# A two-layer hybrid mixer on one core: the first layer's U projection unsplit, norm sums ahead, and a new order of its parts

## The chip, the core and the metric

The kernel runs on one core of a Trainium2 chip. The metric is the device time of one execution in microseconds. Before the change it is 915.59 us, the median of three runs (913.13 to 916.24).

## What is computed

Two layers act on x (256 positions, 1024 channels). Each layer is a hybrid mixer and a gated convolutional feed-forward block, each behind an RMS norm and added to x. Cut to what matters here:

```
h = rmsnorm(x, norm_mix)
u, q, k_cmp, v_cmp, k_sel, v_sel, k_win, v_win, nsa_gate, g_ssm, g_nsa = split(h @ w_in)
y_ssm = s5_mixer(u) @ w_branch_ssm
y_nsa = nsa_mixer(rope(q), ...) @ w_branch_nsa
x = x + (sigmoid(g_ssm) * y_ssm + sigmoid(g_nsa) * y_nsa) @ w_out
x = x + conv_ffn(rmsnorm(x, norm_ffn))
```

The state-space mixer `s5_mixer` runs a linear complex recurrence over 256 steps for 32 groups of 64 states, with a GLU behind it. The attention `nsa_mixer` has 8 query heads on 2 key heads, and adds three softmax branches with gates: over 15 compressed blocks, over selected blocks (all four are selected at this length) and over a window longer than the sequence.

## The kernel before, in words

All activations lie transposed: channels on partitions, 256 positions along the free axis. Weights stream from one packed array `wst` in chunks of 128 x 1024 f32 (512 KB) through a ring of five `raw` buffers (L137, NRAW). Precision is kept in two ways. `split` (L144) turns a chunk into a high part `wh` (ScalarE, L148) and a rest `wl` (VectorE, L150), both fp32r, and `mm3` (L157) adds three fp32r matmuls. In the first layer's mixer most projections instead use the raw chunk in plain f32 matmuls against `xg`, the norm's input times its gain (`proj`, L407); there only U, the state-space input, is split. `split` needs a split input too, `ah` and `al`, made by `Norm.part` (L365, L368).

A norm works as follows: ScalarE squares the eight row blocks of x through one buffer `sq`, VectorE adds them into `nacc`; `finish` (L373) sums over partitions by small matmuls into `ps_n`, does a reciprocal square root in some fifteen tiny VectorE steps (`nt`), spreads it with another matmul, and ScalarE copies it to `rb` (L398). Projections are scaled by `rb` (or by rope tables `rc` that contain it) after the matmul, so matmuls need not wait for the norm.

The first layer's mixer then runs parts that a hand-written list, ORDER[0] (L54), puts in order: `par`, `pf`, `tb` (VectorE: parameters and rotation tables `E` of the recurrence), `q`, `kc`, `ks`, `v` (projections, the first three with rope, whose swapped halves go by DMAs `sw`), `mb` and `mc` (the recurrence's B and C), `cin`, `cw`, `ck`, `cv` (compressed blocks), `ac` and `at` (compressed softmax `sc` and its transpose `ps_ct`), `as` (scores, exponentials), `av` (transposes, values, output `oo`), and `g` (two gate projections and a tanh, eight pairs). A bare number in the list runs that many of sixteen recurrence steps, held in the sequence "A0 B0 A1 C0 B1 D0 A2 C1 B2 D1 A3 C2 B3 D2 C3 D3" (L608): A is the input matmuls `psb` and the products `bc`, `bs`, `z`; B and C are scans of the two halves of time; D the products `pr`, the output matmuls `psy` and the gelu. `gh` is a gate pair that may be issued on TensorE only behind the last attention score traced before it (`gates_held`).

The kernel is written with a tile library. At build time its planner goes through a timeline of its own and gives each engine the ready instruction with the highest priority; priority is the order of the program text. So ORDER sets priorities, and each engine then executes a fixed sequence in order. PSUM has two "mm" banks (projections, gates) and six "aux" banks (the rest). U's first two sums take both "mm" banks, the other two "aux" banks. Later in the mixer x is loaded again into the buffer that q used (L848), on the same SP queue as the weights.

Of the kernel before, what the change touches and what calls it, by code (L numbers as in the profile page):

```python
# [14 lines left out]
T = 256  # L15
# [24 lines left out]
for _name, _w in [("ropec", 256), ("ropes", 256), ("ident", 128), ("causal", 128),  # L40
# [10 lines left out]
NRAW, NWH, NWL, NSS, NSW, NRT, NPT, NZ, NTH = 5, 3, 3, 4, 1, 2, 2, 2, 8  # L51
AHEAD = (3, 4, 5, 6)

ORDER = [[int(x) if x.isdigit() else x for x in o.split()] for o in (  # L54
    ('par tb:0 pf q:1 q:0 mb kc cin tb:1 ks v g:0 1 g:1 cw:0:0 cw:0:1 1 cw:0:2 cw:0:3 1 ck mc 1 g:2 cw:1:0 cw:1:1 1 1 '
     'cw:1:2 cw:1:3 cv g:3 as:0:0 1 ac:0 at:0 1 av:0:0 g:4 as:0:1 1 1 ac:1 at:1 av:0:1 1 as:1:0 1 as:1:1:1 1 gh:5 1 '
     'av:1:0 1 gh:6 av:1:1 1 gh:7 '),
    ('kc mb q:1 1 1 cin 1 cw:0:0 cw:0:1 q:0 ks v 1 cw:0:2 cw:0:3 1 ck cw:1:0 1 ac:0 as:0:0 1 1 cw:1:1 cw:1:2 '
     'cw:1:3 cv g:1 g:2 1 at:0 av:0:0 as:0:1 1 av:0:1 ac:1 as:1:0 1 g:4 1 at:1 as:1:1:1 1 av:1:0 1 g:5 g:7 g:0 1 '
     'g:3 g:6 av:1:1 '))]  # L60
# [22 lines left out]
def body(tc, ctx, d, out):  # L83
# [260 lines left out]
    class Norm:  # L344
        def __init__(self, l, gname, x):
            self.x = x
            self.g = sp(l, gname)
            self.ah = pp.tile([128, KD, T], F32R, name="ah", tag="ah")
            self.al = pp.tile([128, KD, T], F32R, name="al", tag="al")
            self.acc = wk.tile([128, T], F32, name="nacc", bufs=1)  # L350
# [14 lines left out]
        def part(self, k, square=True):  # L365

            gk = self.g[:, k:k + 1]
            S.activation(self.ah[:, k, :], self.x[:, k, :], AF.Copy, scale=gk)  # L368
            stt(self.al[:, k, :], self.x[:, k, :], gk, self.ah[:, k, :].bitcast(F32), OP.mult, OP.subtract)
            if square:  # L370
                self.square(k)
# [29 lines left out]
    def mixer(l, nm, sc, first, mp, sm_):  # L401
        ah, al = nm.ah, nm.al
# [12 lines left out]
        if l == 0:  # L415
            xg = mp.tile([128, KD, T], F32, name="xg", bufs=1)
            for k in range(KD):
                S.activation(xg[:, k, :], nm.x[:, k, :], AF.Copy, scale=nm.g[:, k:k + 1])


        uy = []
        for h in range(2):
            cu = [c or split(l, f"u{2 * h + i}") for i, c in enumerate(first[2 * h:2 * h + 2])]
            psu = [bank("psu", ("mm", "aux")[h]) for _ in range(2)]
            for k in range(KD):
                for i in range(2):
# [99 lines left out]
        def ssm_a(q):  # L526

            Bh, Bl = sv["B"]
            Ec, Es = sv["sc"][:, 0], sv["sc"][:, 1]
            rt = mp.tile([128, 4, TC], F32, name="rm", tag="rm", bufs=1)  # L530
            G.tensor_copy(rt, par[:, R, sl0 + 4 * q:sl0 + 4 * q + 4, None].to_broadcast([128, 4, TC]))
            G.memset(rt[:, :, 0:1], 0.0)
            z = mp.tile([128, 2, 2, 4, TC], F32, name="z", tag="z", bufs=NZ)
            for h in range(2):
                psb = [bank("psb", "aux") for _ in range(2)]
                with row():
                    for c in range(2):
                        for w, y in ((Bh, 0), (Bh, 1), (Bl, 0)):
                            for a in range(2):
                                r = slice(64 * h + 32 * a, 64 * h + 32 * a + 32)  # L540
                                PE.matmul(psb[a][:, c * T:(c + 1) * T], w[r, q, c, :], uy[q][r, y, :],
                                          start=(w is Bh and y == 0), stop=(w is Bl), skip_group_check=True)
                bc = mp.tile([128, 2, 2, 2, TC], F32, name="bc", tag="sb", bufs=2)
                bs = mp.tile([128, 2, 2, 2, TC], F32, name="bs", tag="sb", bufs=2)
                for a in range(2):
                    j = 4 * q + 2 * h + a
                    src = psb[a].rearrange("p (r t) -> p r t", t=TC)
                    for o, e in ((bc, Ec), (bs, Es)):
                        tt(o[:, a].rearrange("p r c t -> p (r c) t"), src,
                           e[:, j, None, :].to_broadcast([128, 4, TC]), OP.mult)  # L550
                for c, op in ((0, OP.add), (1, OP.subtract)):
                    tt(z[:, :, c, 2 * h:2 * h + 2, :].rearrange("p k a t -> p a k t"), bc[:, :, c], bs[:, :, 1 - c], op,
                       eng("z", h))
            st[q] = z, rt
# [23 lines left out]
        def ssm_d(q):  # L578

            z, rt = st.pop(q)  # L580
            Ec, Es = sv["sc"][:, 0], sv["sc"][:, 1]
            Cm = sv["C"]
            psy = bank("psy", "aux")
            for i, (c, e, ci) in enumerate(((0, Ec, 0), (1, Es, 1), (0, Es, 2), (1, Ec, 2))):
                prs = []
                for h in range(2):
                    pr = lt.tile([128, 2, 2, TC], F32, name="pr", tag="ss", bufs=NSS)
                    j = 4 * q + 2 * h
                    tt(pr, z[:, :, c, 2 * h:2 * h + 2, :].rearrange("p k a t -> p a k t"),
                       e[:, j:j + 2, None, :].to_broadcast([128, 2, 2, TC]), OP.mult, eng("pr", 2 * i + h))  # L590
# [17 lines left out]
        ssm = [lambda f=dict(A=ssm_a, B=ssm_b2, C=ssm_c2, D=ssm_d)[o[0]], q=int(o[1]): f(q)  # L608
               for o in "A0 B0 A1 C0 B1 D0 A2 C1 B2 D1 A3 C2 B3 D2 C3 D3".split()]

# [104 lines left out]
        def a_s(qt, ih, alt=0):  # L715
# [4 lines left out]
            Ps = {}  # L720
            if alt:
                pb = [pp.tile([128, 2, 2, T], F32, name="pb", tag=t) for t in ("Bh", "Bl")]
            su = sm_.tile([128, 2, 2, 2], F32, name="su")
            for i2 in range(2):
                i = 2 * ih + i2
                svs = [bank("ps_s", "aux")[:, :2 * nk].rearrange("p (b k) -> p b k", b=2) for _ in range(2)]
                with row():
                    for w, y in ((0, 0), (0, 1), (1, 0)):
                        for kv in range(2):
                            r = slice(64 * kv, 64 * kv + 64)  # L730
                            PE.matmul(svs[kv], q[r, w, i, qs], ksw[r, y, :, :nk], start=(w + y == 0), stop=False,
                                      skip_group_check=True)
                    for kv in range(2):
                        at["hold"] = PE.matmul(svs[kv][:, :, nk - 128:], identb, causb, start=False, stop=True,
                                               skip_group_check=True)
                for kv in range(2):
                    sv = svs[kv]
                    mx = sm_.tile([128, 2], F32, name="mx2", bufs=3)
                    V.tensor_reduce(mx, sv, axis=AX.X, op=OP.max)
                    ts(mx, mx, -SCALE, OP.mult)  # L740
                    pt = pb[kv][:, i2] if alt else lt.tile([128, 2, nk], F32, name="pt", tag="pt", bufs=4)
                    for b in range(2):
                        S.activation(pt[:, b, :], sv[:, b, :], AF.Exp, bias=mx[:, b:b + 1], scale=SCALE,
                                     accum_out=su[:, kv, i2, b:b + 1])
                    Ps[kv, i2] = pt
            V.reciprocal(su, su)
            tt(su, su, gv[:, :, 2 * ih:2 * ih + 2, 1:3], OP.mult)
            for i2 in range(2):
                for kv in range(2):
                    for b in range(2):  # L750
                        S.activation(Ps[kv, i2][:, b, :], Ps[kv, i2][:, b, :], AF.Copy, scale=su[:, kv, i2, b:b + 1])
            at["P", qt, ih] = Ps

        def a_v(qt, ih):
            Ps = at.pop(("P", qt, ih))
# [29 lines left out]
        def gates(m):  # L785
            ps = proj2((f"g{m}", f"g{8 + m}"))
# [5 lines left out]
        def gates_held(m):  # L792

            with tc.issue_after(at["hold"].ins):
                gates(m)

        ssm.reverse()
        run = lambda n: [ssm.pop()() for _ in range(n) if ssm]
        for item in ORDER[l]:
            if isinstance(item, int):  # L800
                run(item)
            else:
                f, *a = item.split(":")
                {"kc": p_kc, "ks": p_ks, "q": p_q, "v": p_v, "cin": c_in, "cw": c_w1, "ck": c_k, "cv": c_v,
                 "par": p_par, "pf": p_pf, "tb": p_tb, "mb": p_mb, "mc": p_mc, "ac": a_cmp, "at": a_cmpt, "as": a_s, "av": a_v, "g": gates, "gh": gates_held}[f](*map(int, a))
        run(99)
# [315 lines left out]
```

## Time and profile before

| what | value |
|---|---|
| median of 3 runs | 915.59 us |
| profiled execution | 911.35 us |
| its span, first to last instruction | 909.6 us |
| TensorE matmul busy | 819.8 us, 90% |
| VectorE busy | 696.8 us, 77% |
| ScalarE busy | 429.4 us, 47% |
| mean granted TensorE clock | 0.94 |

The profile is of one execution. PE is TensorE's matmuls, PEld its weight loads, DVE VectorE, ACT ScalarE, POOL GpSimd, SP the queue that issues most DMAs. "PEclk" or the granted clock is the share of the full TensorE clock that was granted. Shares of the whole span hide that the stages differ; the rows further down are cut by stage. Matmul ends are modelled and overlap, so the price of one in a dense stretch is read from the distance of starts, or from a merged piece divided by its count.

### The profile page before, as it was taken

The page shows a single profiled execution, that of the slowest core. Times are in us where ns is not written, and L with a number is a line of the kernel's source. Part 1 is how long each engine was busy: PE and PEld are TensorE (multiplying, and loading weights), DVE is VectorE, ACT ScalarE, POOL GpSimd, SP SyncE. Part 2 cuts the span into 40 slices and gives each one's busy share as a digit, 9 for nine tenths or more (in the row PEclk, how much of TensorE's full clock was granted, in tenths as well). Part 3 has the DMA queues.
Part 4 walks back from the last instruction along what each step waited for, and adds up shares of the span by engine and source line. Part 5 has one row for each costly group of instructions (what it writes and reads, how often), then busy time and mean ns, then how long its engine had stood idle before and what let it go on. Part 6 is the DMA issues. An engine that isn't in the chain of part 4 may idle for free.

```text
span 909.6 us, 16504 instructions
## 1 busy us (share of the span) xinstructions
PE 819.8 (90%) x6488; PEld 741.9 (82%) x6488; DVE 696.8 (77%) x1337; ACT 429.4 (47%) x795; POOL 29.6 (3%) x58
## 2 busy tenths in 40 slices
PE   4799795789898999999999879997689999999994
PEld 4688574457798999999999748974389999999994
DVE  7975957575499999887784999978468788888553
ACT  6110122455346376565652224776445565655440
POOL 0000100000000000000000122100000000000000
PEclk9899785579999999999999999997899999999997
DMA  7155640024365566665874475332045565555641
GB/s 276 66 168 170 233 147 0 1 76 157 116 177 163 167 194 202 189 193 180 274 245 137 128 270 175 108 125 70 1 139 185 184 201 197 188 197 195 189 136 47
DMA packets 41774, 142.44 MB, mean 157 GB/s; under 512 B 5216, under 2 KB 6752, under 8 KB 41696
## 3 DMA queue, kind: packets, MB, share of 16 engines
q1 hardware_dynamic: 39712, 139.15, 47.7%
q10 hardware_dynamic: 1984, 2.23, 0.9%
q8 instruction: 51, 0.84, 0.4%
q14 instruction: 27, 0.22, 0.1%
HBM read 136.38 MB, written 2.10 MB: 152 GB/s over the span
## 4 chain that ended last, share of the span: by engine, by line
PE 75%; DVE 14%; ACT 4%; DMA 3%; issue 3%; POOL 0%; DVEq 0%; SPq 0%; ACTq 0%
PE ps_f L161 9%; PE ps_f L159 9%; PE ps_f L160 9%; PE ps_g L407 6%; PE ps_fo L160 4%; PE ps_fo L159 4%; PE ps_fo L161 4%; DVE z L561 2%; PE ps_q L407 2%; DMA raw<-wst 2%; PE psy L594 2%; PE ps_g L161 2%; PE ps_br L159 2%; PE ps_br L160 2%; PE ps_br L161 2%
## 5 line engine op out<-in xcount | busy, mean ns | idle before, releaser
L148 ACT CAST wh<-raw 128x1024 fp32r<-128x1024 f32 (+1 forms) x203 | 211.5, 1046 | 215.2 <-PE ps_f L160 96.4
L150 DVE TENSOR_TENSOR wl<-raw,wh 128x1024 fp32r<-128x1024 f32 (+1 forms) x203 | 247.5, 1222 | 64.2 <-ACT wh L148 63.4
L160 PE MATMUL ps_f<-al,wh 128*128 128x256 f32 x704 | 194.5, 276 | 2.3 <-DVE al L203 2.3
L159 PE MATMUL ps_f<-ah,wh 128*128 128x256 f32 x704 | 194.6, 277 | 1.2 <-DVE x L203 1.2
L161 PE MATMUL ps_f<-ah,wl 128*128 128x256 f32 x704 | 194.3, 276 | 0.0
L160 PEld LDWEIGHTS ps_f<-al,wh 128*128 128x128 f32 x704 | 132.2, 188 | 2.5 <-DVE al L203 2.5
L159 PEld LDWEIGHTS ps_f<-ah,wh 128*128 128x128 f32 x704 | 132.2, 188 | 1.3 <-ACT wh L148 1.3
L161 PEld LDWEIGHTS ps_f<-ah,wl 128*128 128x128 f32 x704 | 132.1, 188 | 0.0
L160 PE MATMUL ps_fo<-fl,wh 128*128 128x256 f32 x352 | 97.0, 276 | 0.0
L159 PE MATMUL ps_fo<-fh,wh 128*128 128x256 f32 x352 | 96.9, 276 | 0.0
L161 PE MATMUL ps_fo<-fh,wl 128*128 128x256 f32 x352 | 96.7, 276 | 0.0
L159 PEld LDWEIGHTS ps_fo<-fh,wh 128*128 128x128 f32 x352 | 66.1, 188 | 0.0
L160 PEld LDWEIGHTS ps_fo<-fl,wh 128*128 128x128 f32 x352 | 66.1, 188 | 0.0
L161 PEld LDWEIGHTS ps_fo<-fh,wl 128*128 128x128 f32 x352 | 65.9, 188 | 0.0
L407 PE MATMUL ps_g<-xg,raw 128*128 128x256 f32 x256 | 63.9, 409 | 1.0 <-DMA raw<-wst 1.0
L407 PEld LDWEIGHTS ps_g<-xg,raw 128*128 128x128 f32 x256 | 51.6, 206 | 11.1 <-issue 1.6
L194 DVE TENSOR_TENSOR pr<-z,E 128x512 f32<-128x512 f32 x64 | 41.9, 701 | 15.0 <-PE psy L594 14.9
L203 DVE SCALAR_TENSOR_TENSOR cv<-ab,sp,cv 128x255 f32<-128x255 f32 (+1 forms) x88 | 42.0, 480 | 1.4
L161 PE MATMUL ps_g<-ah,wl 128*128 128x256 f32 x128 | 38.0, 297 | 2.7 <-DVE wl L150 2.7
L561 DVE TENSOR_TENSOR_SCAN z<-rm,z 128x512 f32<-128x512 f32 x32 | 37.9, 1213 | 3.2 <-POOL z L194 3.1
L159 PE MATMUL ps_g<-ah,wh 128*128 128x256 f32 x128 | 37.2, 291 | 0.0
L160 PE MATMUL ps_g<-al,wh 128*128 128x256 f32 x128 | 36.6, 286 | 0.0
(264 smaller groups left out, 1754.5 us busy)
## 6 DMA issues: line engine op xcount, KB each, us to landing
raw<-wst SPq DMA_DIRECT2D x248, 512.0 KB, 4.2
x<-xT SPq DMA_DIRECT2D x4, 512.0 KB, 5.1
raw<-wst SPq DMA_DIRECT2D x4, 420.0 KB, 3.7
xd<-x SPq DMA_DIRECT2D x2, 512.0 KB, 6.9
x<-xd SPq DMA_DIRECT2D x2, 512.0 KB, 7.2
sw<-rt SPq DMA_DIRECT2D x12, 64.0 KB, 3.3
sw<-rt ACTq DMA_DIRECT2D x12, 64.0 KB, 3.4
raw<-wst SPq DMA_DIRECT2D x2, 280.0 KB, 2.7
```

Of the source, the lines that this page charges most:

```text
L148: S.copy(h[:, :n], t[:, :n])
L150: V.tensor_tensor(lo[:, :n], t[:, :n], h.bitcast(F32)[:, :n], op=OP.subtract)
L159: PE.matmul(ps, wh, ah, start=start, stop=False, **k)
L160: PE.matmul(ps, wh, al, start=False, stop=False, **k)
L161: PE.matmul(ps, wl, ah, start=False, stop=stop, **k)
L194: return e.tensor_tensor(o, a, b, op=op)
L203: e.scalar_tensor_tensor(o, a, s, b, op0=op0, op1=op1)
L407: PE.matmul(ps, w[:, k * 128:(k + 1) * 128], xg[:, k, :], start=k == 0, stop=k == KD - 1, skip_group_check=True)
L561: V.tensor_tensor_scan(f, rt.rearrange("p a t -> p (a t)"), f, 0.0, op0=OP.mult, op1=OP.add)
L594: PE.matmul(psy[32 * a:32 * a + 32, :T], Cm[:, ci, 4 * q + a, :], prs[a // 2][:, a % 2].rearrange("p c t -> p (c t)"), start=(i == 0), sto ...
```

## The change

The first layer's U projection uses raw chunks and `xg` in plain f32 like the others, all four sums in "aux" banks; `ah` and `al` are not made for that norm. Its squares come behind the `xg` copies, and its `finish` gets a priority 400 instructions earlier (0 in the second layer). The recurrence steps become named parts in ORDER, and A, D, the scores and the gates are cut in halves that can be placed by themselves. The first layer's order is new; the diff's core:

```diff
+HP = (400, 0)
-ORDER = [[int(x) if x.isdigit() else x for x in o.split()] for o in (
-    ('par tb:0 pf q:1 q:0 mb kc cin tb:1 ks v g:0 1 g:1 cw:0:0 cw:0:1 1 cw:0:2 cw:0:3 1 ck mc 1 g:2 cw:1:0 cw:1:1 1 1 '
-     'cw:1:2 cw:1:3 cv g:3 as:0:0 1 ac:0 at:0 1 av:0:0 g:4 as:0:1 1 1 ac:1 at:1 av:0:1 1 as:1:0 1 as:1:1:1 1 gh:5 1 '
-     'av:1:0 1 gh:6 av:1:1 1 gh:7 '),
-    ('kc mb q:1 1 1 cin 1 cw:0:0 cw:0:1 q:0 ks v 1 cw:0:2 cw:0:3 1 ck cw:1:0 1 ac:0 as:0:0 1 1 cw:1:1 cw:1:2 '
-     'cw:1:3 cv g:1 g:2 1 at:0 av:0:0 as:0:1 1 av:0:1 ac:1 as:1:0 1 g:4 1 at:1 as:1:1:1 1 av:1:0 1 g:5 g:7 g:0 1 '
-     'g:3 g:6 av:1:1 '))]
+ORDER = [o.split() for o in (
+    ('par tb:0 pf q:1 q:0 mb kc cin tb:1 A:0:0 A:0:1 ks B:0 v A:1:0 A:1:1 g:0:0 g:0:1 g:1:0 g:1:1 cw:0:0 cw:0:1 '
+     'C:0 cw:0:2 cw:0:3 ck mc B:1 D:0:0 D:0:1 g:2:0 g:2:1 cw:1:0 cw:1:1 A:2:0 A:2:1 cw:1:2 cw:1:3 cv ac:0 at:0 '
+     'ac:1 as:0:0:0 as:0:0:1 at:1 C:1 g:3:0 g:3:1 B:2 D:1:0 D:1:1 av:0:0 as:0:1:0 as:0:1:1 A:3:0 A:3:1 g:4:0 g:4:1 '
+     'av:0:1 as:1:0:0 as:1:0:1 C:2 g:5:0 g:5:1 B:3 as:1:1:0:1 as:1:1:1:1 D:2:0 D:2:1 av:1:0 g:6:0 g:6:1 C:3 g:7:0 '
+     'g:7:1 D:3:0 D:3:1 av:1:1 '),
+    ('kc mb q:1 A:0:0 A:0:1 B:0 cin A:1:0 A:1:1 cw:0:0 cw:0:1 q:0 ks v C:0 cw:0:2 cw:0:3 B:1 ck cw:1:0 D:0:0 D:0:1 '
+     'ac:0 as:0:0:0 as:0:0:1 A:2:0 A:2:1 C:1 cw:1:1 cw:1:2 cw:1:3 cv g:1:0 g:1:1 g:2:0 g:2:1 B:2 at:0 av:0:0 '
+     'as:0:1:0 as:0:1:1 D:1:0 D:1:1 av:0:1 ac:1 as:1:0:0 as:1:0:1 A:3:0 A:3:1 g:4:0 g:4:1 C:2 at:1 as:1:1:0:1 '
+     'as:1:1:1:1 B:3 av:1:0 D:2:0 D:2:1 g:5:0 g:5:1 g:7:0 g:7:1 g:0:0 g:0:1 C:3 g:3:0 g:3:1 g:6:0 g:6:1 av:1:1 '
+     'D:3:0 D:3:1 '))]
...
+            for k in range(KD):
+                nm.square(k)
...
-            cu = [c or split(l, f"u{2 * h + i}") for i, c in enumerate(first[2 * h:2 * h + 2])]
-            psu = [bank("psu", ("mm", "aux")[h]) for _ in range(2)]
+            cu = [c or (split(l, f"u{2 * h + i}") if l else raw(l, f"u{2 * h + i}"))
+                  for i, c in enumerate(first[2 * h:2 * h + 2])]
+            psu = [bank("psu", "aux" if l == 0 else ("mm", "aux")[h]) for _ in range(2)]
             for k in range(KD):
                 for i in range(2):
+                    if l == 0:
+                        PE.matmul(psu[i][:, :T], cu[i][0][:, k * 128:(k + 1) * 128], xg[:, k, :], start=k == 0,
+                                  stop=k == KD - 1, skip_group_check=True)
+                        continue
                     wh, wl = wt(cu[i], k)
                     mm3(psu[i][:, :T], wh, wl, ah[:, k, :], al[:, k, :], k == 0, k == KD - 1)
             if h == 0:
-                nm.finish()
+                with tc.high_priority(offset=HP[l]):
+                    nm.finish()
...
-        def gates(m):
-            ps = proj2((f"g{m}", f"g{8 + m}"))
+        def gates(m, h=None):
+            if h != 1:
+                th[m] = bank("ps_g")
+            ps = th[m]
+            for i in (0, 1) if h is None else (h,):
+                n = f"g{8 * i + m}"
+                proj(ps[:, i * T:(i + 1) * T], raw(l, n)[0] if l == 0 else split(l, n))
+            if h == 0:
+                return
...
-    nm = Norm(0, "g_mix", x)
-    first = [split(0, "u0")]
+    nm = Norm(0, "g_mix", x, False)
+    first = [raw(0, "u0")]
     nc.sync.dma_start(x[:, 4:8, :], d["xT"][:, 4:8, :])
-    first += [split(0, "u1"), None, None]
+    first += [raw(0, "u1"), None, None]
...
-    for k in range(KD):
-        nm.part(k, False)
-    for k in range(KD):
-        nm.square(k)
```

`ssm_a(q, h)`, `ssm_d(q, h)` and `a_s(qt, ih, i2)` get an argument for the half in the same way; their instructions stay as they are.

## Rows read from the trace of the kernel before

**Rows 1.** Stretches, in us from the start: length, busy time (instructions) per engine, PEclk, DMA.
```profile
0.00:21.00 21.00, 9.19 (x48) 8.19 (x48) 14.91 (x61) 14.17 (x29) 0.20 (x4) 1.00 0.76 271
21.00:35.57 14.57, 7.67 (x61) 7.18 (x61) 12.80 (x96) 1.94 (x5) 0.80 (x2) 0.91 0.29 107
35.57:70.20 34.63, 34.63 (x158) 29.60 (x158) 26.92 (x75) 4.79 (x10) 0.00 (x0) 0.94 0.46 137
70.20:135.00 64.80, 58.52 (x342) 45.32 (x342) 44.77 (x74) 10.36 (x22) 5.14 (x12) 0.89 0.57 187
135.00:195.00 60.00, 39.01 (x221) 24.93 (x222) 41.54 (x91) 21.35 (x76) 2.26 (x10) 0.56 0.00 0
195.00:227.00 32.00, 32.00 (x200) 24.41 (x200) 16.16 (x33) 21.45 (x53) 0.00 (x0) 0.97 0.50 165
227.00:235.00 8.00, 7.93 (x62) 5.25 (x61) 3.92 (x12) 2.37 (x6) 0.00 (x0) 1.00 0.19 66
...
490.00:660.00 170.00, 148.10 (x1191) 117.20 (x1192) 138.16 (x240) 87.25 (x193) 18.24 (x26) 0.93 0.38 121
...
70.20:235.00 164.80, 137.45 (x820) 99.91 (x821) 106.40 (x207) 55.52 (x156) 7.41 (x22) 0.79 0.33 109
```

**Rows 2.** Timeline, 25 to 52 us: start, length, engine, line, operation, idle before and releaser.
```profile
25.78 1.22 DVE L155 TENSOR_TENSOR Bl<-raw,Bh 128x1024 fp32r<-128x1024 f32 x1 [1.77 <-ACT Bh L154]
...
27.16 0.15 DVE L200 TENSOR_SCALAR nt<-ps_n 128x2 f32<-128x2 f32 x1
...
33.58 0.37 ACT L398 COPY rb<-ps_n 128x256 f32<-128x256 f32 x1 [7.84 <-PE ps_n L395]
...
35.57 16.11 PE L407 MATMUL ps_q<-xg,raw 128*128 128x256 f32 x64 [2.02 <-DVE uf L194]
```

**Rows 3.** Groups by line, 0 to 35.57 us: operation, count, busy and mean ns, idle before.
```profile
L150 DVE TENSOR_TENSOR wl<-raw,wh 128x1024 fp32r<-128x1024 f32 x4 | 4.9, 1222 | 0.1
L148 ACT CAST wh<-raw 128x1024 fp32r<-128x1024 f32 x4 | 4.0, 1038 | 0.2 <-DMA raw<-wst 0.2
...
L203 DVE SCALAR_TENSOR_TENSOR al<-x,sp,ah 128x256 fp32r<-128x256 f32 x8 | 3.5, 482 | 0.0
L368 ACT ACTIVATE ah<-x,sp 128x256 fp32r<-128x256 f32 x8 | 3.4, 493 | 0.0
```

**Rows 4.** Timeline of TensorE: split U at two times, one gate pair in plain f32.
```profile
13.31 0.41 PE L160 MATMUL psu<-al,wh 128*128 128x256 f32 x1
...
13.95 0.41 PE L160 MATMUL psu<-al,wh 128*128 128x256 f32 x1
...
19.11 0.28 PE L160 MATMUL psu<-al,wh 128*128 128x256 f32 x1
...
19.45 0.28 PE L160 MATMUL psu<-al,wh 128*128 128x256 f32 x1
...
74.86 7.17 PE L407 MATMUL ps_g<-xg,raw 128*128 128x256 f32 x32
```

**Rows 5.** Chain (first chunk), stretch 5 to 10 us, DMA issues with us to landing.
```profile
1.18 6.19 DMA raw<-wst
...
5.00:10.00 5.00, 0.58 (x1) 0.29 (x1) 3.89 (x16) 3.75 (x9) 0.00 (x0) 1.00 1.02 408
...
raw<-wst SPq DMA_DIRECT2D x248, 512.0 KB, 4.2
```

**Rows 6.** Timeline of ScalarE: two squares in a row.
```profile
5.84 0.40 ACT L357 ACTIVATE sq<-x 128x256 f32<-128x256 f32 x1
...
6.73 0.42 ACT L357 ACTIVATE sq<-x 128x256 f32<-128x256 f32 x1 [0.49 <-DVE nacc L194]
```

**Rows 7.** Waits of TensorE, 60 to 236 us: total, times, longest.
```profile
PE ps_ct L710 <- DVE sc L194: 15.4, 2, 9.5
```

**Rows 8.** Groups by line of TensorE, 195 to 235 us: the gate matmuls.
```profile
L407 PE MATMUL ps_g<-xg,raw 128*128 128x256 f32 x96 | 22.8, 392 | 0.0
```

**Rows 9.** Waits of the SP queue, 0 to 236 us: total, times, longest.
```profile
SPq L848 <- PE ps_s L734: 62.8, 1, 62.8
```

More of the change, by code (lines that the diff above doesn't have):

```diff
@@ L344, in body, with __init__ @@
     class Norm:
-        def __init__(self, l, gname, x):
+        def __init__(self, l, gname, x, split=True):
             self.x = x
             self.g = sp(l, gname)
-            self.ah = pp.tile([128, KD, T], F32R, name="ah", tag="ah")
-            self.al = pp.tile([128, KD, T], F32R, name="al", tag="al")
+            if split:
+                self.ah = pp.tile([128, KD, T], F32R, name="ah", tag="ah")
+                self.al = pp.tile([128, KD, T], F32R, name="al", tag="al")
             self.acc = wk.tile([128, T], F32, name="nacc", bufs=1)
@@ L363, in square, with part @@
                     self.rest = sq
-        def part(self, k, square=True):
+        def part(self, k):
             gk = self.g[:, k:k + 1]
@@ L369, in part @@
             stt(self.al[:, k, :], self.x[:, k, :], gk, self.ah[:, k, :].bitcast(F32), OP.mult, OP.subtract)
-            if square:
-                self.square(k)
+            self.square(k)
         def finish(self):
@@ L401, in mixer @@
     def mixer(l, nm, sc, first, mp, sm_):
-        ah, al = nm.ah, nm.al
+        if l:
+            ah, al = nm.ah, nm.al
         def proj(ps, w):
@@ L524, in mixer, with ssm_a @@
         ys = []
-        def ssm_a(q):
+        def ssm_a(q, h):
             Bh, Bl = sv["B"]
             Ec, Es = sv["sc"][:, 0], sv["sc"][:, 1]
[L530 to L554, printed above, removed]
@@ new lines, in ssm_a @@
+            if h == 0:
+                rt = mp.tile([128, 4, TC], F32, name="rm", tag="rm", bufs=1)
+                G.tensor_copy(rt, par[:, R, sl0 + 4 * q:sl0 + 4 * q + 4, None].to_broadcast([128, 4, TC]))
+                G.memset(rt[:, :, 0:1], 0.0)
+                st[q] = mp.tile([128, 2, 2, 4, TC], F32, name="z", tag="z", bufs=NZ), rt
+            z = st[q][0]
+            psb = [bank("psb", "aux") for _ in range(2)]
+            with row():
+                for c in range(2):
+                    for w, y in ((Bh, 0), (Bh, 1), (Bl, 0)):
+                        for a in range(2):
+                            r = slice(64 * h + 32 * a, 64 * h + 32 * a + 32)
+                            PE.matmul(psb[a][:, c * T:(c + 1) * T], w[r, q, c, :], uy[q][r, y, :],
+                                      start=(w is Bh and y == 0), stop=(w is Bl), skip_group_check=True)
@@ new lines, in ssm_a @@
+            bc = mp.tile([128, 2, 2, 2, TC], F32, name="bc", tag="sb", bufs=2)
+            bs = mp.tile([128, 2, 2, 2, TC], F32, name="bs", tag="sb", bufs=2)
+            for a in range(2):
+                j = 4 * q + 2 * h + a
+                src = psb[a].rearrange("p (r t) -> p r t", t=TC)
+                for o, e in ((bc, Ec), (bs, Es)):
+                    tt(o[:, a].rearrange("p r c t -> p (r c) t"), src,
+                       e[:, j, None, :].to_broadcast([128, 4, TC]), OP.mult)
+            for c, op in ((0, OP.add), (1, OP.subtract)):
+                tt(z[:, :, c, 2 * h:2 * h + 2, :].rearrange("p k a t -> p a k t"), bc[:, :, c], bs[:, :, 1 - c], op,
+                   eng("z", h))
@@ L576, in ssm_c2, with ssm_d @@
             scan(q, 1)
-        def ssm_d(q):
-            z, rt = st.pop(q)
+        def ssm_d(q, h):
+            z, rt = st[q]
             Ec, Es = sv["sc"][:, 0], sv["sc"][:, 1]
             Cm = sv["C"]
-            psy = bank("psy", "aux")
-            for i, (c, e, ci) in enumerate(((0, Ec, 0), (1, Es, 1), (0, Es, 2), (1, Ec, 2))):
+            if h == 0:
+                sv["psy"] = bank("psy", "aux")
+            psy = sv["psy"]
+            for i, (c, e, ci) in list(enumerate(((0, Ec, 0), (1, Es, 1), (0, Es, 2), (1, Ec, 2))))[2 * h:2 * h + 2]:
                 prs = []
-                for h in range(2):
+                for b in range(2):
                     pr = lt.tile([128, 2, 2, TC], F32, name="pr", tag="ss", bufs=NSS)
-                    j = 4 * q + 2 * h
-                    tt(pr, z[:, :, c, 2 * h:2 * h + 2, :].rearrange("p k a t -> p a k t"),
-                       e[:, j:j + 2, None, :].to_broadcast([128, 2, 2, TC]), OP.mult, eng("pr", 2 * i + h))
+                    j = 4 * q + 2 * b
+                    tt(pr, z[:, :, c, 2 * b:2 * b + 2, :].rearrange("p k a t -> p a k t"),
+                       e[:, j:j + 2, None, :].to_broadcast([128, 2, 2, TC]), OP.mult, eng("pr", 2 * i + b))
                     prs.append(pr)
@@ L596, in ssm_d @@
                                   start=(i == 0), stop=(i == 3), skip_group_check=True, tile_position=(0, 32 * a))
+            if h == 0:
+                return
             yf = mp.tile([128, T], F32, name="yf", tag="yf")
@@ L607, in mixer @@
         st = {}
-        ssm = [lambda f=dict(A=ssm_a, B=ssm_b2, C=ssm_c2, D=ssm_d)[o[0]], q=int(o[1]): f(q)
-               for o in "A0 B0 A1 C0 B1 D0 A2 C1 B2 D1 A3 C2 B3 D2 C3 D3".split()]
         kk = []
@@ L713, in a_cmpt, with a_s @@
             at["pcT", qt] = pcT
-        def a_s(qt, ih, alt=0):
+        def a_s(qt, ih, i2, alt=0):
             nk = (qt + 1) * 128
@@ L719, in a_s @@
             gv = gt[:, qt, :].rearrange("p (k h b) -> p k h b", k=2, b=3)
[L720 to L732, printed above, removed]
+            if i2 == 0:
+                pb = [pp.tile([128, 2, 2, T], F32, name="pb", tag=t) for t in ("Bh", "Bl")] if alt else None
+                at["P", qt, ih] = {}, sm_.tile([128, 2, 2, 2], F32, name="su"), pb
@@ L733, in a_s @@
+            Ps, su, pb = at["P", qt, ih]
+            i = 2 * ih + i2
+            svs = [bank("ps_s", "aux")[:, :2 * nk].rearrange("p (b k) -> p b k", b=2) for _ in range(2)]
+            with row():
+                for w, y in ((0, 0), (0, 1), (1, 0)):
                     for kv in range(2):
-                        at["hold"] = PE.matmul(svs[kv][:, :, nk - 128:], identb, causb, start=False, stop=True,
-                                               skip_group_check=True)
+                        r = slice(64 * kv, 64 * kv + 64)
+                        PE.matmul(svs[kv], q[r, w, i, qs], ksw[r, y, :, :nk], start=(w + y == 0), stop=False,
+                                  skip_group_check=True)
@@ L736, in a_s @@
                 for kv in range(2):
[L737 to L744, printed above, removed]
@@ L745, in a_s @@
-                    Ps[kv, i2] = pt
+                    at["hold"] = PE.matmul(svs[kv][:, :, nk - 128:], identb, causb, start=False, stop=True,
+                                           skip_group_check=True)
+            for kv in range(2):
+                sv = svs[kv]
+                mx = sm_.tile([128, 2], F32, name="mx2", bufs=3)
+                V.tensor_reduce(mx, sv, axis=AX.X, op=OP.max)
+                ts(mx, mx, -SCALE, OP.mult)
+                pt = pb[kv][:, i2] if alt else lt.tile([128, 2, nk], F32, name="pt", tag="pt", bufs=4)
+                for b in range(2):
+                    S.activation(pt[:, b, :], sv[:, b, :], AF.Exp, bias=mx[:, b:b + 1], scale=SCALE,
+                                 accum_out=su[:, kv, i2, b:b + 1])
+                Ps[kv, i2] = pt
@@ L746, in a_s @@
+            if i2 == 0:
+                return
             V.reciprocal(su, su)
             tt(su, su, gv[:, :, 2 * ih:2 * ih + 2, 1:3], OP.mult)
-            for i2 in range(2):
+            for j in range(2):
                 for kv in range(2):
                     for b in range(2):
-                        S.activation(Ps[kv, i2][:, b, :], Ps[kv, i2][:, b, :], AF.Copy, scale=su[:, kv, i2, b:b + 1])
-            at["P", qt, ih] = Ps
+                        S.activation(Ps[kv, j][:, b, :], Ps[kv, j][:, b, :], AF.Copy, scale=su[:, kv, j, b:b + 1])
@@ L754, in a_v @@
         def a_v(qt, ih):
-            Ps = at.pop(("P", qt, ih))
+            Ps = at.pop(("P", qt, ih))[0]
             pso = bank("ps_o", "aux")[:, :256]
@@ L783, in mixer @@
         th = {}
-        def gates(m):
-            ps = proj2((f"g{m}", f"g{8 + m}"))
+        def gates(m, h=None):
[5 more added lines that the diff above has]
+                proj(ps[:, i * T:(i + 1) * T], raw(l, n)[0] if l == 0 else split(l, n))
+            if h == 0:
+                return
             t = lt.tile([128, 2, T], F32, name="th", tag="th", bufs=NTH)
@@ L790, in gates, with gates_held @@
             th[m] = t
-        def gates_held(m):
+        def gates_held(m, h=None):
             with tc.issue_after(at["hold"].ins):
-                gates(m)
-        ssm.reverse()
-        run = lambda n: [ssm.pop()() for _ in range(n) if ssm]
+                gates(m, h)
+        parts = {"kc": p_kc, "ks": p_ks, "q": p_q, "v": p_v, "cin": c_in, "cw": c_w1, "ck": c_k, "cv": c_v, "par": p_par,
+                 "pf": p_pf, "tb": p_tb, "mb": p_mb, "mc": p_mc, "ac": a_cmp, "at": a_cmpt, "as": a_s, "av": a_v,
+                 "g": gates, "gh": gates_held, "A": ssm_a, "B": ssm_b2, "C": ssm_c2, "D": ssm_d}
         for item in ORDER[l]:
[L800 to L806, printed above, removed]
+            f, *a = item.split(":")
+            parts[f](*map(int, a))
         zs = []
```

## The prediction

> **What bounds the kernel now.** I read the stretches first: busy time and granted TensorE clock of each stage [rows 1]. The two feed-forward stages lie outside the edits, so I looked only at the two mixers: the first runs from 0 to about 235 us, the second from about 490 to 660. In the first, no engine is full for long. In 21 to 35.57 TensorE works 7.7 of 14.6 us while VectorE works 12.8. In 135 to 195 VectorE works 41.5 of 60 us, TensorE is busy 39.0 at a granted clock of 0.56 (mostly the lower of its two levels, 1.2 GHz), and the DMA queues move nothing. In 195 to 227 TensorE is full and VectorE works 16.2 of 32. So three different things limit this mixer in turn: a late start, a chain of dependencies, and TensorE work kept back for the end.
>
> The timeline shows the late start [rows 2]. TensorE's first `ps_q` matmul begins at 35.57, and had waited for VectorE's `uf`: both "mm" banks held U sums that `uf` must empty. `uf` needs `rb`, the end of the norm's chain, at 33.58. That chain's VectorE steps start at 27.16, behind `Bl`, for which VectorE stood 1.77 us.
>
> The waits and the groups show the other two. TensorE waited 15.4 us in two places for the compressed softmax, `ps_ct` for `sc` [rows 7]. The last 96 gate matmuls, gates 5 to 7, lie after the held point at 195 [rows 8].
>
> **The change, part by part.**
>
> *U unsplit, first layer.* It removes four `wl` and eight `al` from VectorE, 4 x 1.222 + 8 x 0.482 = 8.7 us, and four `wh` and eight `ah` from ScalarE, 4.0 + 3.4 = 7.4 us [rows 3]. On TensorE 32 triples of fp32r matmuls become 32 plain f32 matmuls. A triple took 0.64 us around 13 us (13.31 to 13.95) and 0.34 us around 19 us (19.11 to 19.45; the clock column reads 1.00 for both, so I go by the spacing); a plain f32 matmul took 7.17 / 32 = 0.224 us [rows 4]. The early half-rate price of one is no row: from below 0.224, from above 0.64 (a triple then). I take twice 0.224, 0.45, since the triple also doubled. U can start when `xg` and the second weight chunk are there. The first raw chunk landed at 7.37 and 408 GB/s moved then [rows 5]; 0.6 MB more is some 1.5 us, so about 9 to 10 (estimate). Then 16 x 0.45 + 16 x 0.224 = 10.8 us, so U ends near 21.
>
> There is a rule against this. A plain f32 matmul costs 0.224 us here against 0.34 for the triple. The Trainium skill, FP8 and Floating Point Precision, section TensorE Precision Notes, says true FP32 takes four passes through the array, by which one would cost more than the three passes of the split. By that rule U would end near 32 (worked out under the rivals). The row disagrees with it.
>
> *A queue that this moves.* A raw U buffer was free once `wl` was made; now it is held until its matmuls end. There are five buffers, so the second q chunk is issued only after the first half of U, near 17, and lands some 4.2 us later [rows 5], at 21 to 22. The eight matmuls of the first q chunk (1.8 us) cover that.
>
> *Norm sums first, U sums in "aux".* Squares and adds alternate at 0.89 us each through the one `sq` buffer (5.84 to 6.73) [rows 6], so eight of them after the eight `xg` copies end near 17. The small steps from 27.16 to `rb` took 6.4 us, so `rb` comes at 23 to 25 instead of 34. On TensorE the sums' small matmuls may stand in front of the second half of U by up to a microsecond. What matters more: `ps_q` needs no bank that `uf` must empty. TensorE starts q at about 21, and the start moves by 35.57 - 21 = 14.5 us. VectorE must follow. Up to 70.2, where the first SSM block starts on it, it worked 14.9 + 12.8 + 26.9 = 54.6 us [rows 1]. Less 8.7 that is 45.9, from 5.7, with some 3 us of waits: 54.6, or 15.6 earlier. Both engines agree, so **14.5 us** stands; bounds 10 (VectorE waits as often as before) and 16.
>
> *The order of the first layer.* A moves ahead of `ks`, `v`, the second compressed softmax ahead of the first scores, and gates 5 to 7 lose their hold and stand between attention steps. Nothing is added: the same DMAs, banks and instructions. A takes its copy `rm` on POOL along, which works 7.4 us in all of 70.2 to 235 and so has room. From 70.2 to 235 is 164.8 us, with VectorE 106.4 busy [rows 1]. TensorE's need at full clock is busy time times granted clock: 58.5 x 0.89 + 39.0 x 0.56 + 32.0 x 0.97 = 105, and 8 from 227 to 235: 113 us. Lower bound of the gain: 0, if the chain of waits decides. Upper bound: the second mixer, in which the same blocks lie between dense projections, keeps VectorE at 138.2 / 170 = 81%; 106.4 / 0.81 = 131 us, a gain of 34. The gates that move are 96 x 0.224 = 21.5 us; the time without TensorE work in 135 to 195 is 21 us, and the half clock there adds more. I take **half, 17 us**: the removed hold lets gates fill the gap, but each attention step then stands behind a few gate matmuls in TensorE's order.
>
> *What is late next.* VectorE, with 106 us, and TensorE, with 113, become nearly equal; behind a scan and eight `pr` products an `oo` or `th` step will wait. On the SP queue the reload of `x` stood 62.8 us until the last scores released q [rows 9]; gate weights behind it wait likewise, covered only by what lies in the five buffers.
>
> *Finer parts, and the second layer.* Spelled out, the old numbers in the second layer's order give the very sequence of the new one, and the halves of each part stand next to each other. I cost this at nothing, plus or minus 2 us for a planner that may break ties otherwise. There is no stall there to cover.
>
> **Sum.** 14.5 + 17 = 31.5 us. The profiled execution took 911.35 us, the median is 915.59, so it stands 0.5% below. 911.35 - 31.5 = 879.9 in its terms, 884.0 in terms of the median. With the bounds: gains of 10 + 0 - 2 = 8 to 16 + 34 + 2 = 52, or 864 to 908.
>
> **The rivals.**
>
> *Only the start counts.* The order gives nothing, because the chain from scores to `oo` is as long as before and the gates only change sides. 915.6 - 14.5 = 901. For it: two of the long waits [rows 7] are softmax steps, not TensorE work. Against: the half clock and the empty DMA in 135 to 195.
>
> *It packs fully.* The full 34 us: 915.6 - 48.5 = 867. For it: TensorE and VectorE both have room. Against: the planner's idea of durations and the chip's differ, or 135 to 195 would not have been empty.
>
> *Slower: a bare tail.* Without the hold all gates may be used up before the last scores, and after them the last SSM and attention steps run alone, at half clock. The place is what now is 195 to 235. TensorE has there 39.9 busy, of which gates 21.5; the other 18.4 double to 37, and with VectorE's 20 in series the stretch takes 57 instead of 40, 17 more, while the middle gains nothing. 915.6 - 14.5 + 17 = 918. It decides from a tail of some 54 us on. For it: 135 to 195 is such a stretch. Against: non-gate and gate work is nearly in balance, so gates should last.
>
> *Plain f32 is dear.* Four passes at 0.34 / 3 make 0.453 at full rate and 0.907 at half: 10 + 16 x 0.907 + 16 x 0.453 = 31.8, and the start gains 3.8 us, not 14.5: 915.6 - 3.8 - 17 = 895. The rule is the one named above; rows 4 speak against it.
>
> *It does not do what it says* holds for the finer parts alone, and is in the sum.
>
> **How the numbers follow.** Forecast (874 to 895 as its own range) 0.52, only the start 0.22, full packing 0.16, dear f32 0.02, bare tail 0.08. The predicted time is the likeliest case, 884. The range 866 to 905 leaves out the bare tail (0.08), about half of full packing (0.08) and a sliver of the second case (0.02). A measurement of this kernel can tell 0.3%, 2.7 us. Slower: 0.06 of the bare tail's 0.08. Same: its other 0.02, and 0.02 of the second case. Faster: the rest, 0.90.
>
> **What would show it.** Right: `ps_q` starts near 21; `rb` before 26; the first `bc` near 55; U as 32 f32 matmuls in about 11 us; gate matmuls inside the stretch between the first scores and the last, with a granted clock over 0.8; the second mixer and the feed-forward stages as long as now, within 2 us. Wrong: `ps_q` waits for raw weights; the first `bc` stays beyond 65; a stretch of half clock after the last gate; or the second mixer moves by over 4 us.

## The result, and the profile after

The changed kernel takes 875.96 us, the median of four runs (873.18 to 877.46); the kernel before, measured beside it, takes 915.91. The ratio is 0.9565, 95% interval 0.9531 to 0.9600. The forecast was 884.0, in a range of 866 to 905. The time is inside; the gain is 40 us where 31.5 were forecast, and not all of the forecast's reasons hold.

The page of the changed kernel, its second part: the span in 40 slices of 21.8 us.

```profile
span 871.1 us, 16396 instructions
...
PE   5998999899989999999998889986899999999994
...
PEclk9999999799999999999999899967999999999997
```

The first mixer, now 0 to about 195 us, is the first nine slices. TensorE has a 5 in the first of them and an 8 or 9 in the others, and the granted clock falls once, to 7 in the eighth. The stretches of the changed kernel, 20 us each (columns as in rows 1):

```profile
20.00:40.00 20.00, 20.00 (x96) 17.65 (x96) 18.95 (x103) 2.64 (x5) 0.00 (x0) 1.00 0.61 192
40.00:60.00 20.00, 20.00 (x111) 16.82 (x109) 19.90 (x39) 3.52 (x7) 0.00 (x0) 1.00 0.51 144
60.00:80.00 20.00, 20.00 (x111) 16.73 (x114) 19.93 (x31) 1.29 (x4) 2.09 (x8) 1.00 0.61 198
80.00:100.00 20.00, 15.83 (x128) 10.91 (x120) 14.84 (x25) 4.80 (x9) 1.29 (x5) 0.91 0.68 222
100.00:120.00 20.00, 20.00 (x136) 16.99 (x135) 17.92 (x35) 3.87 (x8) 1.49 (x6) 1.00 0.58 187
120.00:140.00 20.00, 20.00 (x136) 15.75 (x138) 9.64 (x28) 8.75 (x31) 0.00 (x0) 1.00 0.38 114
140.00:160.00 20.00, 20.00 (x140) 14.34 (x132) 14.94 (x32) 13.97 (x37) 0.00 (x0) 1.00 0.45 151
160.00:180.00 20.00, 14.88 (x94) 6.57 (x92) 18.08 (x39) 13.72 (x46) 0.78 (x4) 0.74 0.16 53
180.00:200.00 20.00, 19.99 (x161) 14.73 (x153) 10.93 (x24) 13.06 (x31) 0.00 (x0) 1.00 0.19 54
```

From 20 to 80 us both TensorE (the first number behind the length) and VectorE (the third) are nearly full. In 80 to 100 TensorE waits 4.2 us for ScalarE in the hidden layer of the compressed blocks (`ps_h` for `hs` and `hid`); no run here touches that wait. The same stretch of the kernel before, 60 to 80 us:

```profile
60.00:80.00 20.00, 20.00 (x104) 16.46 (x103) 7.75 (x18) 2.50 (x6) 0.00 (x0) 1.00 0.60 179
```

There VectorE worked 7.75 of 20 us beside a full TensorE. The prediction did not look at this stretch by itself; its rows of 34.6 and 64.8 us, which meet at 70.2, average over the hole. The half clock of 135 to 195 [rows 1] has shrunk to a part of 160 to 180.

The timeline of TensorE and ScalarE in the changed kernel, 8 to 53 us, and VectorE's first `bc`:

```profile
8.77 10.11 PE L437 MATMUL psu<-xg,raw 128*128 128x256 f32 x32 [8.77 <-ACT xg L424]
...
19.53 7.15 PE L437 MATMUL psu<-xg,raw 128*128 128x256 f32 x32
26.52 4.48 PE L413 MATMUL ps_q<-xg,raw 128*128 128x256 f32 x20
30.84 0.61 PE L400 MATMUL ps_n<-dg,ones 128*128 128x128 f32 x4
31.29 9.66 PE L413 MATMUL ps_q<-xg,raw 128*128 128x256 f32 x44
...
31.74 1.05 ACT L159 CAST Bh<-raw 128x1024 fp32r<-128x1024 f32 x1 [16.93 <-DMA raw<-wst]
32.70 0.37 ACT L403 COPY rb<-ps_n 128x256 f32<-128x256 f32 x1
...
52.21 1.28 DVE L199 TENSOR_TENSOR bc<-psb,E 128x512 f32<-128x512 f32 x2
```

q starts at 26.52 instead of 35.57 [rows 2], without waiting for `uf`, and the first `bc` at 52.21 instead of 70.2. But U leaves 64 records in the trace, not 32, and `rb` comes at 32.70, hardly before the 33.58 of before.

### The profile page after: what moved, and what is told of

Read it like the earlier page. It is cut to its first block, busy times and chain, and to the rows that moved or that the text cites. A ratio compares the mean times of both kernels' runs of the same rounds, so it can differ in the third digit from the quotient of the medians.

```text
span 871.1 us, 16396 instructions
## 1 busy us (share of the span) xinstructions
PE 808.7 (93%) x6456; PEld 733.6 (84%) x6456; DVE 689.6 (79%) x1325; ACT 421.6 (48%) x783; POOL 25.4 (3%) x58
## 4 chain that ended last, share of the span: by engine, by line
PE 76%; DVE 14%; DMA 3%; ACT 3%; issue 3%; POOL 0%; ACTq 0%; DVEq 0%; SPq 0%
PE ps_f L165 9%; PE ps_f L166 9%; PE ps_f L164 9%; PE ps_g L413 5%; PE ps_fo L166 5%; PE ps_fo L165 5%; PE ps_fo L164 5%; DVE z L575 3%; PE psu L437 2%; PE ps_g L165 2%; PE ps_br L164 2%; PE ps_g L166 2%; PE ps_br L165 2%; PE ps_br L166 2%; PE ps_g L164 2%
## 5 line engine op out<-in xcount | busy, mean ns | idle before, releaser
L153 ACT CAST wh<-raw 128x1024 fp32r<-128x1024 f32 (+1 forms) x199 | 207.4, 1046 | 219.8 <-PE ps_f L165 99.0
L155 DVE TENSOR_TENSOR wl<-raw,wh 128x1024 fp32r<-128x1024 f32 (+1 forms) x199 | 242.6, 1221 | 66.7 <-ACT wh L153 66.1
L413 PE MATMUL ps_g<-xg,raw 128*128 128x256 f32 x256 | 59.8, 389 | 0.0
L413 PEld LDWEIGHTS ps_g<-xg,raw 128*128 128x128 f32 x256 | 48.6, 194 | 8.0 <-issue 1.2
```

The lines of the kernel that those rows point to most:

```text
L153: S.copy(h[:, :n], t[:, :n])
L155: V.tensor_tensor(lo[:, :n], t[:, :n], h.bitcast(F32)[:, :n], op=OP.subtract)
L413: PE.matmul(ps, w[:, k * 128:(k + 1) * 128], xg[:, k, :], start=k == 0, stop=k == KD - 1, skip_group_check=True)
```

## The experiments

Each is the changed kernel with one edit, if nothing else is said. Differences between them are differences of ratios to the kernel before, times 916 us; each ratio is good to about 0.35%, 3 us, so two of them that differ by less than some 4.5 us (3.2 times the root of 2) are not told apart. Rows of a trace are of one execution each.

**Old order** (e1).

```diff
-    ('par tb:0 pf q:1 q:0 mb kc cin tb:1 A:0:0 A:0:1 ks B:0 v A:1:0 A:1:1 g:0:0 g:0:1 g:1:0 g:1:1 cw:0:0 cw:0:1 '
...
+    ('par tb:0 pf q:1 q:0 mb kc cin tb:1 ks v g:0:0 g:0:1 A:0:0 A:0:1 g:1:0 g:1:1 cw:0:0 cw:0:1 B:0 cw:0:2 cw:0:3 '
...
```

> The changed kernel with the first layer's old order (the same fine parts, gates 5 to 7 held again). If start and order each bring their own share and add up (about 15 us from the start, as the first bc moved from 70.2 to 55.3, and about 24 from the order): 901 us, 894 to 906. If the order brings nothing and all comes from the start: 876. If the start brings nothing by itself, because the old order's chain decides: 914 to 917.

Measured: 897.56 us, ratio 0.980 (0.9766 to 0.9834). The start alone brings 18 us, the order another 21.5 on top. The first `bc` starts at 58.9, so the start alone moves it by 11.3 us (in the changed kernel it starts at 52.21; the expectation's 55.3 is not that row).

**New order alone** (e2): the kernel before with the new order.

```diff
-    nm = Norm(0, "g_mix", x, False)
-    first = [raw(0, "u0")]
+    nm = Norm(0, "g_mix", x)
+    first = [split(0, "u0")]
...
-            psu = [bank("psu", "aux" if l == 0 else ("mm", "aux")[h]) for _ in range(2)]
+            psu = [bank("psu", ("mm", "aux")[h]) for _ in range(2)]
...
```

> The kernel before with the first layer's new order alone: U split, sums in mm and aux banks, squares and finish as before. If the shares add up: 915.9 - 24 = 892 us, 886 to 898. If the order needs the early start: over 905. If the start brings nothing: 876 to 880.

Measured: 885.57 us, ratio 0.9654 (0.9612 to 0.9696): 32 us from the order alone. That is just outside the range for shares that add up, and clear of the other two. The shares do not add: 18 + 32 = 50 against 40. The first `bc` starts at 62.2, 8.0 us earlier than before. With the order in place, the start is worth only 8 us more.

**Gates 5 to 7 held again** (e3).

```diff
-     'av:0:1 as:1:0:0 as:1:0:1 C:2 g:5:0 g:5:1 B:3 as:1:1:0:1 as:1:1:1:1 D:2:0 D:2:1 av:1:0 g:6:0 g:6:1 C:3 g:7:0 '
-     'g:7:1 D:3:0 D:3:1 av:1:1 '),
+     'as:1:0:0 as:1:0:1 C:2 B:3 as:1:1:0:1 as:1:1:1:1 gh:5:0 gh:5:1 D:2:0 D:2:1 av:1:0 gh:6:0 gh:6:1 C:3 gh:7:0 '
+     'gh:7:1 D:3:0 D:3:1 av:1:1 '),
```

> The changed kernel, with gates 5 to 7 held behind the last scores again and put behind them in the order. If spreading the gates is what the order brings: about 21 us of gate work returns to the tail and the half clock to the stretch before it, 890 to 900 us. If the gain of the order is the SSM and compressed blocks ahead: 876 to 881.

Measured: 882.62 us, ratio 0.9624 (0.9586 to 0.9662), some 5 us lost; its interval still touches that of the changed kernel. Between the two expectations, nearer the second. Its stretches show that the gates do fill a gap:

```profile
140.00:160.00 20.00, 12.78 (x72) 6.94 (x73) 16.06 (x30) 9.72 (x41) 0.77 (x4) 0.74 0.00 1
160.00:180.00 20.00, 20.00 (x120) 15.37 (x117) 12.24 (x27) 14.88 (x42) 0.00 (x0) 0.92 0.52 159
```

TensorE works 12.8 of 20 us in 140 to 160, at a granted clock of 0.74, where the changed kernel is full at 1.00; it is full behind it instead.

**Old order, gates not held** (e4): e1 with `g:5`, `g:6`, `g:7` for `gh:5`, `gh:6`, `gh:7`.

> The changed kernel with the first layer's old order, but gates 5 to 7 without their hold. If spreading the gates is what the order brings: 876 to 886 us. If it is the SSM and compressed blocks ahead: as with the old order and the hold, within 5 us. If unheld gates leave a bare tail in the old order: slower than with the hold.

Measured: 897.85 us, ratio 0.9807 (0.9766 to 0.9848), the same as with the hold. So in the old order spreading the gates is worth nothing, although they do fill the gap that they were meant for. TensorE's wait for the compressed softmax, 60 to 236 us, in e1 and here (total, times, longest):

```profile
PE ps_ct L725 <- DVE sc L199: 18.4, 2, 12.2
...
PE ps_ct L725 <- DVE sc L199: 2.0, 1, 2.0
```

The gap moves behind the gates. The last gate matmuls, the last scores, and the stretches between:

```profile
134.34 13.61 PE L413 MATMUL ps_g<-xg,raw 128*128 128x256 f32 x54
...
192.80 0.61 PE L749 MATMUL ps_s<-causb,identb 128*128 128x256 bf16 x2
...
160.00:180.00 20.00, 14.59 (x101) 9.73 (x93) 11.10 (x28) 8.13 (x20) 0.00 (x0) 0.59 0.00 1
180.00:200.00 20.00, 15.24 (x66) 6.34 (x65) 19.44 (x39) 9.90 (x37) 0.78 (x4) 0.50 0.16 53
```

This is the bare tail of the rivals: 45 us from the end of the last gate, 147.95, to the last scores, at half clock from 160 on. In e1 the last scores come at 176.97. So the tail costs what the spread gates win.

**SSM blocks late** (e9).

```diff
-    ('par tb:0 pf q:1 q:0 mb kc cin tb:1 A:0:0 A:0:1 ks B:0 v A:1:0 A:1:1 g:0:0 g:0:1 g:1:0 g:1:1 cw:0:0 cw:0:1 '
...
+    ('par tb:0 pf q:1 q:0 mb kc cin tb:1 ks v g:0:0 g:0:1 A:0:0 A:0:1 g:1:0 g:1:1 cw:0:0 cw:0:1 B:0 cw:0:2 cw:0:3 '
...
```

> The changed kernel with only the SSM blocks (A0, B0, A1, C0, B1, D0, A2 and D1) back at their old places among ks, v, the first gates, the compressed blocks and the scores; the compressed blocks stay ahead and gates 5 to 7 spread. If what the order brings is VectorE work in 60 to 80 us, where VectorE worked 10.9 of 20 us with the old order and 19.9 with the new: the hole of some 9 to 12 us is back, 885 to 892 us. If it is the compressed blocks ahead: 876 to 880.

Measured: 890.12 us, ratio 0.9732 (0.9702 to 0.9761), 15 us lost, clear of the changed kernel's interval. The hole is back, and the work turns up late:

```profile
60.00:80.00 20.00, 19.56 (x118) 15.54 (x116) 10.92 (x16) 1.28 (x3) 0.78 (x4) 1.00 0.59 174
...
140.00:160.00 20.00, 17.09 (x136) 12.04 (x136) 19.00 (x45) 8.88 (x35) 0.77 (x4) 1.00 0.35 124
160.00:180.00 20.00, 11.01 (x57) 6.25 (x55) 18.91 (x30) 9.57 (x29) 1.50 (x6) 0.57 0.00 1
180.00:200.00 20.00, 15.92 (x109) 7.71 (x110) 13.89 (x35) 17.73 (x55) 0.00 (x0) 0.83 0.17 54
```

VectorE works 10.9 of 20 us in 60 to 80 instead of 19.9, and up to 80 us it has done 59.5 us of work instead of 71.4. From 140 to 200 it works 51.8 us instead of 44.0, and in 160 to 180 TensorE has 11.0 to do instead of 14.9, at a granted clock of 0.57. This is the largest part of the order. The edit also moves B2 and A3 back by a place or two, which the expectation does not name.

**Compressed softmax late** (e8).

```diff
-     'ac:1 as:0:0:0 as:0:0:1 at:1 C:1 g:3:0 g:3:1 B:2 D:1:0 D:1:1 av:0:0 as:0:1:0 as:0:1:1 A:3:0 A:3:1 g:4:0 g:4:1 '
...
+     'as:0:0:1 C:1 g:3:0 g:3:1 B:2 D:1:0 D:1:1 av:0:0 as:0:1:0 as:0:1:1 ac:1 at:1 A:3:0 A:3:1 g:4:0 g:4:1 av:0:1 '
...
```

> The changed kernel with the second compressed softmax (ac:1, at:1) back behind the first values, as before. If the SSM blocks ahead are what counts: 876 to 880 us. If TensorE's waits for the compressed softmax (15.4 us in two places before) are what the order removes: 884 to 892.

Measured: 880.00 us, ratio 0.9627 (0.9591 to 0.9662): some 6 us by the ratios, 4 by the medians, at the edge of what can be told: the upper end of the first range, short of the second. TensorE's waits for the compressed softmax do not come back with this edit, so it does not price them. The first softmax (`ac:0`, `at:0`), which the new order puts ahead of the first scores, was put back by itself in no run.

**U's sums in the "mm" banks** (e5).

```diff
-            psu = [bank("psu", "aux" if l == 0 else ("mm", "aux")[h]) for _ in range(2)]
+            psu = [bank("psu", ("mm", "aux")[h]) for _ in range(2)]
```

> The changed kernel with U's first two sums in the mm banks again. q then waits for uf, near 37 us in place of 26. If TensorE's early start is what the start brings: 5 to 10 us are lost, 881 to 887. If VectorE's saved 8.7 us are: 876 to 879.

Measured: 874.71 us, ratio 0.9563 (0.9527 to 0.9598), no difference that can be told. q does wait for `uf`, but `uf` is early:

```profile
25.74 0.71 PE L400 MATMUL ps_n<-dg,ones 128*128 128x128 f32 x4
28.48 14.08 PE L413 MATMUL ps_q<-xg,raw 128*128 128x256 f32 x64 [2.03 <-DVE uf L199]
...
26.49 0.37 ACT L403 COPY rb<-ps_n 128x256 f32<-128x256 f32 x1 [11.88 <-PE ps_n L400]
```

`rb` is there at 26.49, 6.2 us before the changed kernel's, since no q matmuls stand in front of `ps_n` on TensorE. q loses 2 us, not 10.

**U split, the rest as changed** (e6): `split` and `mm3` for U again, with `ah` and `al`; banks, squares and priority stay.

> The changed kernel with U split as before, but aux banks, squares after xg and early finish kept. A plain f32 U takes 64 matmul records of 0.224 us, 14.3 us at full clock, against 10.9 us for the split, so TensorE gains 3.4 us and more at half clock; VectorE and ScalarE get 8.7 and 7.4 us back. If VectorE decides: 882 to 887. If TensorE decides: 869 to 874.

Measured: 880.25 us, ratio 0.9620 (0.9586 to 0.9655), some 5 us lost, at the edge of what can be told and between the two ranges. The sign is that of VectorE and ScalarE, though U has less to do on TensorE when split. The run does not tell these two apart, nor from what the split does to the norm: its sums start on TensorE at 25.10 instead of 18.72, and `rb` comes at 36.84 instead of 32.70.

**No earlier priority** (e7), and **neither banks nor priority** (e10).

```diff
-                with tc.high_priority(offset=HP[l]):
-                    nm.finish()
+                nm.finish()
```

> The changed kernel without the earlier priority of the norm's finish. In the changed kernel rb came at 32.70 us, hardly before the 33.58 of the kernel before, so if the early start is the banks' and the unsplit U's doing, the priority is worth nothing: 874 to 879 us. If the priority carries the start: 880 to 886.

> U's first two sums in the mm banks and no earlier priority of finish, the rest as changed. If either of the two is enough to let q start early (with mm banks and the priority q started at 28.48, with aux banks at 26.52), taking both away brings the wait of q for uf back: q after 32, 880 to 886 us. If neither matters because U unsplit alone frees the engines: 874 to 879.

Measured: e7 872.43 us, ratio 0.9536 (0.9503 to 0.9568); e10 877.82 us, 0.9583 (0.9523 to 0.9644). Neither can be told from the changed kernel, and in e10 q started at 28.32, not after 32. So neither the priority nor the banks carry the 5 to 10 us that were set down for them. Smaller shares stay open: the first `ps_br`, behind the first mixer, comes at 206.9 (e5) and 208.3 (e10) with the "mm" banks, at 202.6 (e7) and 200.0 (changed kernel) with the "aux" banks, but the medians (e5 1.3 us below the changed kernel, e10 1.9 above) do not bear that lead out.

**Later SSM blocks forward too** (e11), and **that without the priority** (e12).

```diff
-     'C:0 cw:0:2 cw:0:3 ck mc B:1 D:0:0 D:0:1 g:2:0 g:2:1 cw:1:0 cw:1:1 A:2:0 A:2:1 cw:1:2 cw:1:3 cv ac:0 at:0 '
+     'cw:0:2 cw:0:3 ck mc B:1 D:0:0 D:0:1 A:2:0 A:2:1 g:2:0 g:2:1 cw:1:0 cw:1:1 C:1 B:2 cw:1:2 cw:1:3 cv ac:0 at:0 '
...
```

> The changed kernel with the later SSM blocks moved forward too (A2 ahead of gate 2, C1 and B2 ahead of the last compressed weights, D1 and A3 ahead of gate 3, C2 and B3 one place). If VectorE's holes are what is left (4.2 of 10 us worked in 120 to 130, 5.4 in 130 to 140): 866 to 871 us. If TensorE, which is full from 90 to 160 us, limits that stretch: 873 to 880. If the attention chain behind the blocks pays: over 881.

> The changed kernel with the later SSM blocks forward and without the earlier priority of finish. If the two small differences seen with each alone (874.4 and 872.4 us against 876.0) are real and add up: 868 to 872 us. If they are scatter around a stretch that TensorE fills: 873 to 878, the same as the changed kernel.

Measured: e11 874.37 us, ratio 0.9549 (0.9524 to 0.9575); e12 872.68 us, 0.9543 (0.9518 to 0.9567). In e11 VectorE works 14.3 of 20 us in 120 to 140 instead of 9.6, where TensorE was full anyway, and the granted clock of 160 to 180 reads 1.00 instead of 0.74; still nothing that can be told is won. No version tried beats the changed kernel clearly.

## Why the prediction was right or wrong

**U on TensorE: wrong.** The step took "a plain f32 matmul took 7.17 / 32 = 0.224 us". The 32 are records of the trace, not matmuls. The code issues 16 matmuls for a gate pair and 32 for U; the trace shows 32 and 64. A plain f32 matmul leaves two records and costs 0.437 us (the second half of U begins at 19.53 and q at 26.52: 6.99 us for 16 matmuls). Three fp32r matmuls cost 0.34 [rows 4], so unsplitting U makes TensorE's work longer. The Trainium skill, FP8 and Floating Point Precision, section TensorE Precision Notes, has four passes for true FP32; an estimate from that, at 0.34 / 3 a pass, is 0.453, and the measurement agrees within 4%. The prediction's "the row disagrees with it" came from the count of records. Its times of whole pieces, such as the 21.5 us of the gates, are not touched by this; the eight matmuls of the first q chunk are 3.5 us, not 1.8. The rival "plain f32 is dear", given 0.02, had the price right and the end of U too late: 31.8 forecast, 26.7 measured. U began at 8.77 and its first half took 10.1 us, not 14.5: up to 14.00 its records stood 0.44 us apart (12 of them), behind that 0.24 (20 up to 18.72).

**The start: its size near, by another way.** TensorE's q moved by 9.05 us, not 14.5. VectorE's first `bc` moved by 18.0, where 15.6 were worked out, but that is start and order together: the start alone moved it by 11.3 us (e1), the order alone, with A ahead of `ks` and `v`, by 8.0 (e2). In time the start is worth 18 us under the old order and 8 under the new one, so that 14.5 lies between them is in part luck. e6 puts some 5 of the 8 on U unsplit. The squares behind the `xg` copies were taken back by themselves in no run.

**Norm sums and banks: wrong in both halves.** `rb` was forecast for 23 to 25 and came at 32.70. The squares were done by 14.8, earlier than the 17 worked out, but their small matmuls stood behind the first half of U on TensorE (18.72 to 19.67). `dg`, the input of the matmul that spreads them, was ready at 26.7; that matmul stood behind 20 q records in TensorE's fixed order, until 30.84, and the copy behind the `Bh` cast on ScalarE. With no q records in front `rb` came at 26.49 (e5). "What matters more: `ps_q` needs no bank" is not borne out: e5 and e10 lose nothing that can be told.

**The order: right in sign, short in size, wrong in its main reason.** 17 us were forecast, from gates that fill the gap of 135 to 195. Measured: 21.5 on top of the start, 32 alone. Taken back one at a time, the SSM blocks are worth 15, the compressed softmax some 6 and the gates some 5 (26 together; they overlap). Against the prediction's reason stands e4: gates without hold, in the old order, fill the wait for the compressed softmax and bring 0. The hole that counted was VectorE's in 60 to 80, beside a TensorE that was full: e9 brings it back and loses 15. From the end of the last gate to the last scores it is 45 us in e4, 34 in e9 (150.3 to 184.3) and 15 in the changed kernel (153.3 to 168.0). So with the SSM blocks early the bare tail is short, and then spreading the gates is worth its 5 us (e3); that the one needs the other is read from these traces, and no run tests it by itself.

**Finer parts and the second layer: right in the main, one stage not.** No run takes the finer parts alone. In the second mixer the landmarks `rc` and last `ps_o` of compressed values moved by 40.6 and 40.1 us, so between them it changed by 0.5 us. But the first mixer gained more than the kernel did: the first `ps_br` behind it moved by 44.2 us (244.2 to 200.0), the end of the span by 38.5. Of the difference, 3.5 us were given back in the first feed-forward stage: from its first `ps_f` to its first `ps_fo` the trace before has 123.9 us and the trace after 127.4, with a granted clock of 0.94 instead of 1.00 in the first 31 us. Another 1.7 went between that `ps_o` and the last `ps_br`. The sign "as long as now, within 2 us" failed there. The other runs have 123.9 to 125.8 us in that feed-forward stage, so it may be scatter; the cause is open.

**The rivals.** "Only the start counts" forecast 901; the run with the start alone took 897.6, the change did not stop there. The bare tail, with half clock after the last gate, exists for part of 160 to 180, and in e4 for longer. Full packing was forecast at 867; the kernel came to within 9 us of it.

## What to carry to other kernels

Cut the stretches of a profile fine enough that a hole on the second engine shows beside a full first one; work that only waits for its place in the order belongs there. A gap that is filled can open again behind what filled it (e4), so look at when the last step of the chain comes. Parts of a start and of an order that fill the same hole do not add: price each with the other in place. And count matmuls in the code before dividing a busy time by the records of a trace.

## What was not expected of the hardware

A plain f32 matmul of 128 x 128 by 256 appears as two records 0.22 us apart, 0.44 us in all, 1.3 times three fp32r matmuls. By e6 it still paid to use it, by some 5 us at the edge of what can be told, for what VectorE and ScalarE no longer do. And the clock column of a stretch read 1.00 [rows 1, first row] while the fp32r matmuls in it stood at twice their later distance (0.64 and 0.34 us for three) [rows 4]: at the beginning of a trace the distance of starts is the better clock.
